# One selection group of four tiles split into two pairs, in a one-core sparse-attention and state-space layer

## The chip, the cores and the metric

The kernel runs on one core of a Trainium2 chip. The time is device microseconds of one execution. The engines are TensorE (PE), VectorE (DVE), ScalarE (ACT), GpSimd (POOL) and SyncE (SP, which here only issues transfers).

## The reference

The layer projects x (4096 rows of 1024) with one matrix. One part of the columns feeds a sparse attention with 8 heads, one a state-space branch; the gated results are projected back, added to x and normalised. What matters here is how the attention picks its keys:

```
idx_logits  = einsum('bthd,bsd->bths', qi, ki)             # 8 index heads of 32
index_score = einsum('bths,bth->bts', relu(idx_logits), wi)
index_score = where(causal, index_score, neg)
_, sel = top_k(index_score, 256)                           # per query
s = where(valid, q_lat . c[sel], neg); p = softmax(s); o = p . c[sel]
```

The kernel doesn't gather. For every query it finds which 256 visible keys have the largest index score, writes a mask of large numbers for all others to DRAM, and the attention adds that mask to dense scores.

## The kernel before

The 4096 queries are 32 tiles of 128. Tile i sees W = 128 (i + 1) keys. The program has four stages: the projections, the selection (which is put in among the projections), the attention with the state-space work beside it, and the output.

**Projections.** x comes in 8 chunks of 512 rows. A sweep multiplies one chunk with the column blocks: first the three blocks that the selection needs, for all chunks, and then, in eight more sweeps, the rest (u, q, two gates). Each of these sweeps ends with "kv", which splits the latent (ch, cl at the tile names qh, ql), makes four k tiles and four v tiles and stores them in eight parts. All these results go through a tile named st with 3 buffers.

**Selection.** `select(group)` (L285 on) takes a group of tiles. It scores each one (`score`: TensorE products of the 8 index heads, L254; ScalarE's relu, L256; VectorE's weighted accumulation into acc, L265), estimates a threshold from mean and spread, and then does 8 rounds (6 for groups of small tiles). In a round every tile of the group is counted once: how many of its scores lie at or above its threshold. A count runs on VectorE (L329, written to a scratch tile mk) or on ScalarE (L325, as a sum of signs, scratch tile junk_a); which engine takes which tile is read from a table of letters, D and A, in `counters`. Then a chain of short VectorE operations on one number a tile (L331 to L367) moves all thresholds of the group together. After the rounds the masks are made, one tile after the other: a sign step on ScalarE (L386), two passes (L390, L391), a maximum (L393) and a match-replace (L401) on VectorE, the mask in pieces of 2048 columns on ScalarE (L405), and its store on SP.

What can overlap is set by buffers: mk and junk_a have one buffer each, acc has four of 4240 columns, into which several tiles of a group are packed, and the small tiles of a group (s_...) have two.

**Order.** The groups run in the order of the list ORDER (L147 to L150). A scheduler that simulates the program fixes the order of the instructions on each engine when the kernel is built; the engines then run them in that order. So a change in a group moves instructions of the sweeps beside it as well. `cm` and `ca` hold, for each tile, the factors that turn a count or a sum of signs into the same quantity; they are filled by the same table.

**After it.** VectorE sums flags that say whether any tile lost a key (L1013 to L1025), TensorE adds them over the lanes (L1027), and all engines read the sum and branch around an exact selection that is only wanted when it isn't zero (L1029, L1030). Attention follows with an order that is written out by hand for PE, DVE and ACT. While the selection ends and once the last sweep has freed its memory, GpSimd prepares the first two batches of the state-space branch (L815 to L863).

Of the kernel before, what the change touches and what calls it, by code (L numbers as in the profile page):

```python
# [71 lines left out]
def tile_hymba(  # L72
# [74 lines left out]
    SMALL = [[2, 3, 4, 5, 6], [7, 8, 9]]  # L147
    MIDDLE = [[i, i + 1, 30 - i, 31 - i] for i in (14, 12)]
    LARGE = [[i, i + 1] for i in range(30, 21, -2)]
    ORDER = SMALL + MIDDLE + LARGE + [[10, 11, 20, 21]]  # L150
    PLACE = {i: k for k, i in enumerate([0, 1] + [i for g in ORDER for i in g])}
    ROOM = P * (NT + 1) + 16
    SB, XB, KB = 2, 5, 8
# [3 lines left out]

    def counters(group, it):
        p = PAT[len(group)]
        return p[it % len(p)]  # L160

    idxs = ctx.enter_context(ExitStack())
    one = idxs.enter_context(tc.tile_pool(name="i_one", bufs=1))
# [28 lines left out]
    DVE.memset(ca, -AIM)  # L192
    for g in ORDER:
        for r in range(2):
            for i, by in zip(g, counters(g, 2 * r)):
                if by == "A":
                    k = slice(PLACE[i], PLACE[i] + 1)
                    POOL.memset(cm[:, r, k], -0.5)
                    POOL.memset(ca[:, r, k], 0.5 * (P * (i + 1)) - AIM)
# [71 lines left out]
    def causal_only(i):  # L271
        W = P * (i + 1)
        m = wk.tile([P, PEN], BF, name="m", bufs=2)
        if W > P:
            DVE.memset(m[:, :W - P], 0.0)
        DVE.tensor_scalar(m[:, W - P:W], capm, 0.0, BIG, op0=OP.is_lt, op1=OP.mult)
        store_mask(i, m, 0, W)
# [13 lines left out]
    def select(group):  # L291
# [29 lines left out]
        for it in range(rounds):  # L321
            for (k, i, v, W), by in zip(tiles, counters(group, it)):
                if by == "A":
                    junk = wk.tile([P, S], mybir.dt.int8, name="junk_a", bufs=1)
                    ACT.activation(junk[:, :W], v[:, :W], AF.Sign, scale=-1.0, bias=th[:, k:k + 1],  # L325
                                   accum_out=ct[:, k:k + 1])
                else:
                    junk = wk.tile([P, PEN], BF, name="mk", bufs=1).bitcast(mybir.dt.uint8)
                    DVE.tensor_scalar(junk[:, :W], v[:, :W], th[:, k:k + 1], None, op0=OP.is_ge, op1=OP.add,  # L329
                                      accum_out=ct[:, k:k + 1])  # L330
# [122 lines left out]
    with ExitStack() as ph:  # L453
# [339 lines left out]
        causal_only(1)  # L793
        for g in ORDER:
            select(g)
# [212 lines left out]
    lost = one.tile([P, NT], FT, name="lost")  # L1008
    NG = len(ORDER)
    lo1 = one.tile([P, NG + 1], FT, name="lo1")  # L1010
# [11 lines left out]
    DVE.tensor_scalar(lost, lost, 0.0625, None, op0=OP.is_gt)  # L1022
    for r, g in enumerate(ORDER):
        DVE.tensor_reduce(lo1[:, r:r + 1], lost[:, PLACE[g[0]]:PLACE[g[0]] + len(g)], axis=AX.X, op=OP.add)
# [5 lines left out]
    with tc.If(n_lost != 0):  # L1030
        for r, g in enumerate(ORDER):
            g_lost = nc.values_load(lo2[:1, r:r + 1], min_val=0, max_val=5 * P)
# [11 lines left out]
    with ExitStack() as ph:  # L1044
# [195 lines left out]
        with tc.manual_schedule(engines={PE_E, DVE_E, ACT_E}):  # L1240
            for n in range(-AHEAD, len(values)):
                if n + AHEAD < len(values):
                    p, b, want = values[n + AHEAD]
# [20 lines left out]
                if n >= 0:  # L1264
                    p, b, _ = values[n]
# [150 lines left out]
```

## Time and profile before

| | us |
|---|---|
| median of 3 runs | 4118.75 (4113.29 to 4124.88) |
| profiled execution | 4111.49 |
| its span | 4109.7 |
| last projection matmul ends | 1667.0 |
| attention's first loads are issued | 1793.4 |

Busy over the span: PE 90%, DVE 80%, ACT 68%, POOL 38%. All times below count from the start of the span. In the page's forty slices, one slice is 102.7 us; the selection and the projections fill the first seventeen and the attention most of the others. A line of the view in order of time gives the start, the duration, the engine, the line of the program, the operation, the tiles it writes and reads, and the shape; in brackets stands how long the engine was idle before and what ended that.

### The profile page before, as it was taken

The numbers are of one execution on the slowest core, as the hardware profiler recorded it, in microseconds if no ns is written. First come the engines' busy times: TensorE is split into PE (matmuls) and PEld (weight loads), VectorE is DVE, ScalarE is ACT, GpSimd is POOL, SyncE is SP. The second block draws the span as 40 slices with busy tenths as digits, with TensorE's granted clock in tenths as the row PEclk, the third lists the DMA queues.
The fourth block names the chain that finished last, engine by engine and source line by source line (L and its number), as shares of the span: only waits on it lengthen the run. The fifth ranks groups of instructions, "written<-read, shape, count | busy, mean of one in ns | idle before, by whom it ended". The sixth has DMA issues, their size and how long they took to land.

```text
span 4109.7 us, 64216 instructions
## 1 busy us (share of the span) xinstructions
PE 3683.6 (90%) x20925; PEld 3111.3 (76%) x20925; DVE 3298.1 (80%) x6879; ACT 2804.1 (68%) x4540; POOL 1545.4 (38%) x3405
## 2 busy tenths in 40 slices
PE   6788988988989989149999999999999999899998
PEld 5566766766757658038888898888898989788887
DVE  5898898888798888778888888888888889565554
ACT  4587878776767776647777777777777778534342
POOL 1110011111111111236665656666656542354543
PEclk9889989989989899569999999999999999999999
DMA  8766967767668677244545444444444444644441
GB/s 226 159 195 177 307 190 213 200 183 221 190 188 230 185 202 203 71 141 117 154 120 149 124 136 137 128 136 127 140 132 135 119 142 121 181 135 134 143 124 72
DMA packets 521898, 656.19 MB, mean 160 GB/s; under 512 B 126800, under 2 KB 367952, under 8 KB 521552
## 3 DMA queue, kind: packets, MB, share of 16 engines
q1 hardware_dynamic: 438800, 448.54, 37.7%
q0 software_dynamic: 82752, 203.45, 18.5%
q8 instruction: 167, 2.74, 0.3%
q14 instruction: 179, 1.47, 0.1%
HBM read 480.61 MB, written 169.13 MB: 158 GB/s over the span
## 4 chain that ended last, share of the span: by engine, by line
PE 45%; ACT 3%; DMA 3%; issue 2%; DVE 2%; POOL 2%; SPq 0%; ACTq 0%; POOLq 0%; DVEq 0%
PE ps_t L1149 10%; PE ps_o L1161 6%; PE ps_o L1162 5%; PE ps_s L1116 5%; PE ps_s L1117 5%; PE ps_y L99 2%; PE ps_y L98 2%; PE ps_y L100 2%; ACT sc L1132 2%; PE ps L959 2%; PE ps_g L99 1%; PE ps_g L100 1%; PE ps_g L98 1%; DMA mb<-mask_d 1%; ACT ph L85 1%
## 5 line engine op out<-in xcount | busy, mean ns | idle before, releaser
L87 DVE TENSOR_TENSOR pl<-ps_t,ph 128x512 fp32r<-128x512 f32 x1088 | 748.5, 689 | 194.2 <-ACT ph L85 181.1
L85 ACT ACTIVATE ph<-ps_t 128x512 fp32r<-128x512 f32 x1088 | 644.2, 596 | 372.6 <-PE ps_t L1149 353.8
L1119 DVE CUSTOM_DVE_ANT_0 sc<-ps_s,mb 128x512 f32<-128x512 f32 (+3 forms) x1152 | 725.6, 638 | 39.2 <-PE ps_s L1117 18.2
L1161 PE MATMUL ps_o<-ph,V 128*128 128x256 f32 x2176 | 659.3, 325 | 29.9 <-ACT ot L1165 27.0
L1149 PE MATMUL ps_t<-ident,sc 128*128 128x128 f32 x4352 | 655.7, 273 | 10.5 <-DVE pl L87 6.0
L256 ACT ACTIVATE relu<-ps_i 128x1024 f32<-128x1024 f32 (+5 forms) x624 | 534.6, 899 | 168.8 <-PE ps_i L254 147.2
L1132 ACT ACTIVATE sc<-sc,mx 128x1024 f32<-128x1024 f32 (+7 forms) x640 | 637.0, 997 | 7.3 <-DVE mx L1119 7.0
L1149 PEld LDWEIGHTS ps_t<-ident,sc 128*128 128x128 f32 x4352 | 537.0, 141 | 122.6 <-DVE pl L87 6.6
L265 DVE SCALAR_TENSOR_TENSOR acc<-relu,wi,acc 128x2048 f32<-128x2048 f32 (+15 forms) x322 | 558.1, 1733 | 77.2 <-ACT relu L256 74.3
L1162 PE MATMUL ps_o<-pl,V 128*128 128x256 f32 x2176 | 565.0, 282 | 2.6 <-DVE pl L87 2.6
L511 POOL DMA_DIRECT2D w<-w_d x294 | 159.0, 541 | 1085.9 <-PE ps_x L100 1005.8
L98 PE MATMUL ps_x<-xk,w 128*128 128x512 f32 x1280 | 517.1, 404 | 6.5 <-DVE st L87 2.0
L100 PE MATMUL ps_x<-xk,w 128*128 128x512 f32 x1280 | 507.3, 396 | 0.0
L99 PE MATMUL ps_x<-xk,w 128*128 128x512 f32 x1280 | 506.5, 396 | 0.0
L254 PE MATMUL ps_i<-kst,qst 128*128 128x512 f32 (+1 forms) x1136 | 394.9, 446 | 117.2 <-ACT relu L256 111.2
L1116 PE MATMUL ps_s<-KT,QH 128*128 128x512 f32 (+2 forms) x1152 | 438.2, 381 | 19.6 <-DMA V<-v_d 15.2
L1161 PEld LDWEIGHTS ps_o<-ph,V 128*128 128x128 f32 x2176 | 413.5, 190 | 47.4 <-ACT ot L1165 39.5
L1117 PE MATMUL ps_s<-KT,QL 128*128 128x512 f32 (+2 forms) x1152 | 436.4, 379 | 0.7 <-DVE QL L87 0.7
L1162 PEld LDWEIGHTS ps_o<-pl,V 128*128 128x128 f32 x2176 | 417.6, 192 | 7.3 <-DVE pl L87 3.3
L254 PEld LDWEIGHTS ps_i<-kst,qst 128*128 128x128 f32 x1136 | 222.1, 213 | 223.9 <-ACT relu L256 185.7
L325 ACT ACTIVATE junk_a<-acc,s_t 128x1920 int8<-128x1920 f32 (+14 forms) x152 | 333.1, 2191 | 53.8 <-DVE s_t L354 24.1
L98 PEld LDWEIGHTS ps_x<-xk,w 128*128 128x128 f32 x1280 | 245.7, 192 | 70.5 <-DMA w<-w_d 6.2
(408 smaller groups left out, 7435.4 us busy)
## 6 DMA issues: line engine op xcount, KB each, us to landing
w<-w_d POOLq DMA_DIRECT2D x294, 512.0 KB, 4.2
mb<-mask_d SPq DMA_DIRECT2D x416, 256.0 KB, 3.1
xs<-in_x_dram SPq DMA_DIRECT2D x120, 256.0 KB, 4.6
w_d<-w SPq DMA_DIRECT2D x42, 512.0 KB, 4.3
qs_d<-st SPq DMA_DIRECT2D x64, 256.0 KB, 3.0
k_d<-st SPq DMA_DIRECT2D x128, 128.0 KB, 2.4
v_d<-st SPq DMA_DIRECT2D x64, 256.0 KB, 3.5
QL<-qT_d SPq DMA_DIRECT2D x64, 256.0 KB, 4.2
```

The costliest lines, as they stand in the source:

```text
L85: ACT.activation(hi, src, AF.Copy, scale=scale)
L87: DVE.tensor_tensor(lo, src, ft(hi), op=OP.subtract)
L98: PE.matmul(ps, lh, rh, start=first, stop=False)
L99: PE.matmul(ps, lh, rl, start=False, stop=False)
L100: PE.matmul(ps, ll, rh, start=False, stop=last)
L1116: PE.matmul(ps[:, :nn], QH[:, qs], kk, start=True, stop=False)
L1117: PE.matmul(ps[:, :nn], QL[:, qs], kk, start=False, stop=True)
L1119: DVE.tensor_tensor_reduce(self.sc[a][-1][:, o], ps[:, :n], self.mb[a][:, o], 1.0, TOP, OP.add, OP.min, mx[:, k:k + 1])
L1132: ACT.activation(v, v, AF.Exp, scale=-1.0, bias=nm, accum_out=self.ds[:, a, r:r + 1])
L1149: PE.transpose(pt[:, e, a, :], self.sc[a][r][:, o:o + P], ident)
L1161: PE.matmul(self.po, v, ph_[:, e, :], start=(b + e == 0), stop=False)
L1162: PE.matmul(self.po, v, pl_[:, e, :], start=False, stop=(b + e == self.nb - 1))
```

## The change

The last group of the selection, of the tiles 10, 11, 20 and 21, becomes two groups, 20 and 21 first and then 10 and 11. `counters` gives both of them the first entry of the table for pairs, "DA", in every round: the first tile of the pair is counted on VectorE, the second on ScalarE. Before, the group of four had "AAAD" in every round: 10, 11 and 20 on ScalarE, 21 on VectorE. Other pairs have "DA", "DA", "AA" in turn.

```
-    ORDER = SMALL + MIDDLE + LARGE + [[10, 11, 20, 21]]
+    ORDER = SMALL + MIDDLE + LARGE + [[20, 21], [10, 11]]
 ...
     def counters(group, it):
         p = PAT[len(group)]
-        return p[it % len(p)]
+        return p[0 if group in ORDER[-2:] else it % len(p)]
```

How this moves instructions is shown at three places. A width of 1408 belongs to tile 10, 1536 to 11, 2688 to 20 and 2816 to 21.

First place, VectorE, the stretch where the last scores of the selection are accumulated. Before, the last accumulation of tile 21 (its last 768 columns) comes ahead of round 0's count:

```order
L265 SCALAR_TENSOR_TENSOR acc<-relu,wi,acc 128x768 x2
L87 TENSOR_TENSOR st<-ps_x,st 128x512
L265 SCALAR_TENSOR_TENSOR acc<-relu,wi,acc 128x768
L87 TENSOR_TENSOR st<-ps_x,st 128x4x64
L266 TENSOR_TENSOR acc<-acc,capm 128x128
L329 TENSOR_SCALAR mk,s_t<-acc,s_t 128x2816
L87 TENSOR_TENSOR st<-ps_x,st 128x4x64
L331 TENSOR_TENSOR s_t<-s_t,cm 128x4
```

Now the last accumulations are tile 11's, and round 1's count of tile 20 stands among them (round 0's is further up, behind the maximum of tile 23):

```order
L354 TENSOR_TENSOR s_t<-s_ab,s_e 128x2
L87 TENSOR_TENSOR st<-ps_x,st 128x4x64
L265 SCALAR_TENSOR_TENSOR acc<-relu,wi,acc 128x1536
L329 TENSOR_SCALAR mk,s_t<-acc,s_t 128x2688
L265 SCALAR_TENSOR_TENSOR acc<-relu,wi,acc 128x1536
L87 TENSOR_TENSOR st<-ps_x,st 128x4x64
L331 TENSOR_TENSOR s_t<-s_t,cm 128x2
L266 TENSOR_TENSOR acc<-acc,capm 128x128
L304 BN_STATS s_st<-acc 128x6
L332 TENSOR_TENSOR s_t<-s_t,ca 128x2
L87 TENSOR_TENSOR st<-ps_x,st 128x4x64 x2
```

The splits of the v parts (L87, 128x4x64) stand between the short operations of a round in both orders, round 0's before and round 1's now.

Second place, VectorE, from the masks of tiles 20 and 21 into the rounds of 10 and 11, in the changed kernel. Before, no count stands behind a mask pass here:

```order
L401 MATCH_REPLACE acc<-s_top,acc 128x2696
L391 TENSOR_TENSOR acc<-acc,mk 128x768
L393 MAX s_top<-acc 128x8
L329 TENSOR_SCALAR mk,s_t<-acc,s_t 128x1408
L397 TENSOR_TENSOR eq_114<-s_top 128x7
L331 TENSOR_TENSOR s_t<-s_t,cm 128x2
L398 SCALAR_TENSOR_TENSOR s_eqj,tf<-slot_111,s_e,eq_114 128x8
L400 COPY_PREDICATED s_top<-s_tm,spare 128x8
L332 TENSOR_TENSOR s_t<-s_t,ca 128x2
L401 MATCH_REPLACE acc<-s_top,acc 128x2824
```

Round 0 of the small pair begins inside the masks of the large one; its other rounds follow behind them.

Third place, ScalarE, the end of the selection. Before, the last round and the masks of four tiles:

```order
L325 ACTIVATE junk_a,s_t<-acc,s_t 128x1408
L325 ACTIVATE junk_a,s_t<-acc,s_t 128x1536
L325 ACTIVATE junk_a,s_t<-acc,s_t 128x2688
L386 ACTIVATE acc<-acc,s_sg 128x1408
L386 ACTIVATE acc<-acc,s_sg 128x1536
L386 ACTIVATE acc<-acc,s_sg 128x2688
L386 ACTIVATE acc<-acc,s_sg 128x2816
L405 ACTIVATE m,fl<-acc,s_bi,s_sc 128x1408
L405 ACTIVATE m,fl<-acc,s_bi,s_sc 128x1536
```

Now:

```order
L325 ACTIVATE junk_a,s_t<-acc,s_t 128x2816 x6
L325 ACTIVATE junk_a,s_t<-acc,s_t 128x1536
L386 ACTIVATE acc<-acc,s_sg 128x2688
L386 ACTIVATE acc<-acc,s_sg 128x2816
L405 ACTIVATE m,fl<-acc,s_bi,s_sc 128x2048
L405 ACTIVATE m,fl<-acc,s_bi,s_sc 128x640
L405 ACTIVATE m,fl<-acc,s_bi,s_sc 128x2048
L405 ACTIVATE m,fl<-acc,s_bi,s_sc 128x768
L325 ACTIVATE junk_a,s_t<-acc,s_t 128x1536 x7
L386 ACTIVATE acc<-acc,s_sg 128x1408
L386 ACTIVATE acc<-acc,s_sg 128x1536
```

Seven of tile 11's eight counts stand behind the four mask pieces of tiles 20 and 21. Behind the branch the order on PE and ACT is the same in both.

## Rows read from the trace of the kernel before

**Rows 1.** The page: its head, TensorE's share, and TensorE in forty slices.
```profile
span 4109.7 us, 64216 instructions
PE 3683.6 (90%) x20925; PEld 3111.3 (76%) x20925; DVE 3298.1 (80%) x6879; ACT 2804.1 (68%) x4540; POOL 1545.4 (38%) x3405
PE   6788988988989989149999999999999999899998
```

**Rows 2.** TensorE in order of time, from the last projection to the flags.
```profile
1666.37 0.63 PE L100 MATMUL ps_x<-w,ql 128*128 128x512 f32 x1
1787.18 0.20 PE L1027 MATMUL ps_i<-lo,ones 128*1 128x11 f32 x2 [120.18 <-DVE lo L1025]
```

**Rows 3.** VectorE in order of time: counts of rounds 0 to 3, one later round.
```profile
1667.48 3.15 DVE L329 TENSOR_SCALAR_CACHE_REDUCE mk<-acc,s_t 128x2816 uint8<-128x2816 f32 x1
...
1684.42 3.13 DVE L329 TENSOR_SCALAR_CACHE_REDUCE mk<-acc,s_t 128x2816 uint8<-128x2816 f32 x1
...
1694.22 3.15 DVE L329 TENSOR_SCALAR_CACHE_REDUCE mk<-acc,s_t 128x2816 uint8<-128x2816 f32 x1
...
1703.00 3.15 DVE L329 TENSOR_SCALAR_CACHE_REDUCE mk<-acc,s_t 128x2816 uint8<-128x2816 f32 x1
...
1719.20 3.15 DVE L329 TENSOR_SCALAR_CACHE_REDUCE mk<-acc,s_t 128x2816 uint8<-128x2816 f32 x1
...
1725.21 0.16 DVE L331 TENSOR_TENSOR s_t<-s_t,cm 128x4 f32<-128x4 f32 x1 [2.86 <-ACT junk_a L325]
...
1727.30 3.15 DVE L329 TENSOR_SCALAR_CACHE_REDUCE mk<-acc,s_t 128x2816 uint8<-128x2816 f32 x1
```

**Rows 4.** ScalarE in the same later round: tiles 11 and 20, last reading.
```profile
1720.85 1.57 ACT L325 ACTIVATE junk_a<-acc,s_t 128x1536 int8<-128x1536 f32 x1
1722.33 0.19 ACT L325 ACTIVATION_READ_ACCUMULATOR junk_a<-acc,s_t 128x1 f32 x1
1722.55 2.54 ACT L325 ACTIVATE junk_a<-acc,s_t 128x2688 int8<-128x2688 f32 x1
1724.99 0.19 ACT L325 ACTIVATION_READ_ACCUMULATOR junk_a<-acc,s_t 128x1 f32 x1
```

**Rows 5.** VectorE: the last round's count, first mask steps, last match-replace.
```profile
1735.39 3.15 DVE L329 TENSOR_SCALAR_CACHE_REDUCE mk<-acc,s_t 128x2816 uint8<-128x2816 f32 x1
...
1742.29 0.17 DVE L372 TENSOR_SCALAR s_m<-s_ab 128x4 f32<-128x4 f32 x1
...
1744.33 0.95 DVE L390 TENSOR_SCALAR mk<-acc,s_t 128x1408 bf16<-128x1408 f32 x1 [0.38 <-ACT acc L386]
...
1776.66 3.08 DVE L401 MATCH_REPLACE8 acc<-s_top,acc 128x2824 f32<-128x2824 f32 x1
```

**Rows 6.** ScalarE: the four sign steps, the end of the last mask.
```profile
1742.83 7.89 ACT L386 ACTIVATE acc<-acc,s_sg 128x1408 f32<-128x1408 f32 x4 [1.46 <-DVE s_sg L379]
...
1782.83 0.19 ACT L405 ACTIVATION_READ_ACCUMULATOR m<-acc,s_bi,s_sc 128x1 f32 x1
```

**Rows 7.** VectorE by line and shape up to 1790 us: busy us, mean ns.
```profile
L329 DVE TENSOR_SCALAR_CACHE_REDUCE mk<-acc,s_t 128x2560 uint8<-128x2560 f32 x8 | 23.0, 2878 | 0.2
...
L265 DVE SCALAR_TENSOR_TENSOR acc<-relu,wi,acc 128x640 f32<-128x640 f32 x14 | 12.3, 880 | 7.0 <-ACT relu L256 6.9
...
L329 DVE TENSOR_SCALAR_CACHE_REDUCE mk<-acc,s_t 128x1152 uint8<-128x1152 f32 x6 | 8.4, 1406 | 0.1
```

**Rows 8.** Last sweep: ScalarE's split of the latent, VectorE's last v split.
```profile
1647.39 0.63 ACT L85 ACTIVATE qh<-st 128x512 fp32r<-128x512 f32 x1 [2.18 <-DMA st<-c_d]
...
1690.43 0.42 DVE L87 TENSOR_TENSOR st<-ps_x,st 128x256 fp32r<-128x256 f32 x1
```

**Rows 9.** GpSimd and VectorE beside each other; busy us from 1675 to 1700.
```profile
1674.68 2.34 POOL L817 TENSOR_TENSOR U<-U,Uh 128x1024 fp32r<-128x1024 f32 x1
1674.71 2.40 DVE L344 SCALAR_TENSOR_TENSOR s_ab<-s_t,s_e 128x4 f32<-128x4 f32 x2
...
1675.00:1700.00 25.00, 0.00 (x0) 0.00 (x0) 19.37 (x39) 12.54 (x15) 14.02 (x16) 0.50 0.18 52
```

**Rows 10.** The same view: PE, PEld, DVE, ACT, POOL, clock, DMA share, GB/s.
```profile
1500.00:1600.00 100.00, 86.87 (x340) 66.03 (x341) 78.09 (x145) 70.30 (x83) 12.94 (x23) 0.91 0.68 183
```

## The prediction

> **What bounds the kernel now.** I read the page first. Its span is 4109.7 us, TensorE is busy for 90% of it, and its forty slices stand at 6 to 9 tenths except for one, the seventeenth, with 1 [rows 1]. That hole is the place of this change: the last projection matmul runs at 1666.37, and the next thing TensorE does is the small sum over the loss flags at 1787.18, after 120 us of waiting for VectorE [rows 2]. Attention can't begin before a branch that reads those flags, so every microsecond of the selection's end is on the path. What fills the hole is read on VectorE and ScalarE in order of time. The last group of four tiles counts eight rounds: counts on VectorE begin at 1667.48, 1684.42, 1694.22, 1703.00 and then every 8.10 us [rows 3]. In each round ScalarE is the longer side (tiles 10, 11 and 20 one after the other; VectorE's count of tile 21 is over sooner), and then a chain of short VectorE operations, 2.09 us from 1725.21 to 1727.30, moves the thresholds [rows 3, 4]. After round 7 the masks are made: 1742.29 to 1783.02, mostly VectorE with one tile after the other [rows 5, 6].
>
> **The change part by part.** The rounds get shorter, but there are twice as many, and the order on VectorE and ScalarE says that the two pairs don't overlap: all of pair 20/21's rounds come first, then its masks, and the first count of tile 10 stands behind tile 20's match-replace and tile 21's maximum; ScalarE has seven of its eight counts of tile 11 behind the four mask pieces of 20 and 21. Each count on VectorE writes a scratch tile of one buffer (mk) that the masks use too, and each count on ScalarE another of one buffer, so the next group can't count while this one does. I therefore add the pairs up in sequence.
>
> Count times: VectorE takes 1.406 us for 1152 columns and 2.878 for 2560, so 1.045 ns a column: 1.67 for tile 10 (1408) and 3.01 for tile 20 (2688) [rows 7]. ScalarE takes 1.70 for tile 11 from start to start, and 2.63 for 2688 columns with the reading of the sum [rows 4]; tile 21's 2816 are 2.74.
> - A round of 20/21: VectorE is longer, 3.01 and 0.1 to its reading, then the chain 2.09: 5.2 us.
> - A round of 10/11: both sides about 1.78, chain 2.09: 3.87 us.
> - Round 2 has 0.7 us more of short operations (8.78 against 8.10), round 1 about 0.9 (an estimate: the same five operations in one chain), and after round 7 the way to the masks is 1.2 shorter (6.90 from 1735.39 to 1742.29) [rows 3, 5].
>
> From the start of round 2's count of the last large tiles, before: 48.1 us to the masks, and 40.7 for them, 88.8 in all [rows 3, 5, 6]. After, on the same path:
> - rounds 2 to 7 of 20/21: 6 x 5.2 + 0.7 - 1.2 = 30.7;
> - masks: the VectorE work from the first is-ge to the end of the last match-replace is the same 35.4 (1744.33 to 1779.74), now in two pieces, each with a start that waits for ScalarE's sign step. For tile 10 that is 2.0, as before; for tile 20 it is 3.1, since its 2688 columns are 2.5 of the 7.9 us of the four [rows 5, 6];
> - round 0 of 10/11 inside the masks of tile 21: the count 1.7 and 0.3 of short operations. Then ScalarE must write tile 21's mask, 3.4 us (the 3.3 from the end of the match-replace to the end of the last piece, and a gap), before it can count tile 11 again [rows 5, 6]; the 17 short operations of round 0, 2.7 us at 0.16 each, lie beside that [rows 3];
> - rounds 1 to 7 of 10/11: 7 x 3.87 + 0.9 + 0.7 - 1.2 = 27.5;
> - the last mask, of tile 11, one piece of 1536 columns that I take at its count's 1.70 and a gap: 1.8, where tile 21's two pieces took 3.3 [rows 4].
> Sum: 30.7 + 3.1 + 35.4 + 2.0 + 2.0 + 3.4 + 27.5 + 1.8 = 105.9. That is 17.1 us more than before, if round 2 of the large pair starts when it did.
>
> It starts somewhat earlier, which is where the change gains. Rounds 0 and 1 of 20/21 are now counted while tiles 10 and 11 are still being scored: the new order has round 0 right behind the masks of 22/23, and round 1 seven eighths through tile 11's accumulations. Before, rounds 0 and 1 took 26.7 us in the open (1667.48 to 1694.22) [rows 3]. But they are not free. Round 1's chain stands on VectorE behind the splits of the last sweep's v tiles; the last of them began 43.0 us after that sweep's latent was split (1647.39 to 1690.43) [rows 8], since each waits for a store to free one of three buffers. And the accumulations now stand later: where the masks of 22/23 begin, the old order has already scored 1408 + 1536 + 2688 + 512 columns a head and the new one 2688 + 2816, so 640 columns times eight heads, 8 x 0.88 = 7.0 us of VectorE, are still to do at that point [rows 7]. Going down the new order from there by the durations of the old run, I get the last v split at 1685 to 1691 and round 2 some 2.5 us behind it, by its twelve or so short operations. I take 1691 for round 2, 3 us earlier than before, so the net is 17.1 - 3 = **14 us slower**. The bounds of this term: the old chain of round 0 held up the last v splits by at most the 8.8 us that it was longer than a later round (16.9 against 8.1) [rows 3]. Without that they end at 1682, round 2 starts at 1684, and 5 us sooner if the 7.0 us above were not needed in the open: 1679, or +2. The other end is 1701, +24, from GpSimd:
>
> When the sweep frees its memory, GpSimd prepares the first state-space batches; it was busy for 14.0 of the 25 us from 1675. Short VectorE operations beside it stretch: two at L344, four numbers a lane, took 2.40 together while a GpSimd subtraction took 2.34 [rows 9]. A count, with one tensor input, took 3.13 beside GpSimd at 1684.42, no longer than at 1719.20 without it [rows 3]. In the new order the GpSimd operations meet accumulations of tile 11 (L265, two tensor inputs) and round 1's chain instead of round 0's. In the 1691 I have counted 4 us of their 14 as exposed, the rest beside VectorE's wait for the v splits; all 14 exposed is 1701. The Trainium skill (GPSIMD Engine Reference, 1. Specifications) says that GpSimd's SBUF interfaces are shared with VectorE and contend with its instructions that have two SBUF inputs. The rows of L344 agree; by that rule the long accumulations are hit too, which is the upper end just given.
>
> The skill (VectorE: DVE Perf Modes, Mode 2×_2P) also has a rule that speaks against my round: an operation on one fp32 tensor with a scalar may read through both ports, two results a cycle. The is-ge at L390 does (0.95 us for 1408 columns), the count at L329 does not (1.12 ns a column) [rows 3, 5]. If the count of 2688 columns were halved, ScalarE would set the round, 4.9 instead of 5.2, and the sum fall by 2 us; the row decides.
>
> Behind the branch PE and ScalarE have the same order as before, so I cost the rest at nothing. One more group in the flags is one more short reduce. GpSimd's spread for 10/11 (L307) now stands among its state-space operations, but its result is wanted only after the masks of 20 have begun, and SP's mask stores are in the order of the masks: nothing for either. Everything ahead of the masks of 22/23 is reordered too, since the scheduler reacts to each shift; the trace can't price that. In the 100 us from 1500, TensorE was busy 86.9 and VectorE 78.1 us [rows 10], so there is slack that a new order can gain or lose; I allow 8 us either way.
>
> **Its own time.** The profiled execution took 4111.49 us, 1.8 more than its span and 7.3 below the median of the runs, 4118.75. On its terms the forecast is 4125.5; against the median, with the same 14 us, 4132.
>
> **Rivals.**
> 1. *The large pair is hidden altogether.* Round 2 starts by 1683: the v splits go faster without the old chain in front of them. For it: the old stall of 8 us in that chain. Against: 43 us for the sweep's end, which is no VectorE matter alone. Price: +2 to +6, 4121 to 4125 against the median.
> 2. *Faster, because scoring ends sooner.* With 20 and 21 scored first, the remaining scores are short tiles whose work fits between the sweep's matmuls; the stretch to 1667 shrinks. Break-even is round 2 at 1677, a gain past 0.3% needs it before 1665. For it: the idle tenths of TensorE in the first sixteen slices [rows 1]. Against: the sweep's matmuls are unchanged and all 22/23 work stands in front as before. Price: about -15, 4104.
> 3. *GpSimd and the accumulations in turn.* All 14 us of GpSimd work fall between VectorE operations: round 2 at 1701, +24, 4143. For it: VectorE has no pause in that part of the new order. Against: its waits for the v splits, 16.9 us of stretch and wait together before [rows 3].
> 4. *The pairs overlap after all*, so that one's chain lies beside the other's count. A double round would be about 3.1 + 1.8 + 2.1 = 7 us, six of them 42 instead of 48, masks 2 longer, the start 3 earlier: -7, 4112. The written order speaks against it on both engines.
>
> **How the numbers follow.** Forecast 0.60 (its own range +6 to +22), rival 1 0.17, rival 2 0.08, rival 3 0.12, rival 4 0.03. A difference below 0.3%, 12.4 us, can't be told from none. Slower by more: the part of the forecast above 12.4 us, six tenths of it, 0.36, and rival 3, so 0.48. Within: 0.24 + 0.17 + 0.03 = 0.44. Faster: 0.08. The range reaches from -6 to +28 around the median, 4113 to 4147: it leaves out rival 2 and the far end of rival 3.
>
> **What would show it.** In the profile after: VectorE counts of 2688 columns 5.2 us apart and then, some 31 us after the last of them began, counts of 1408 columns 3.9 us apart; two separate stretches of match-replace; TensorE idle from its last projection for 130 to 140 us instead of 120; round 2 of the large pair near 1691. I am wrong if counts of the two pairs alternate, if that round starts before 1680, or if the last projection matmul moves by more than 10 us from 1666.

## The result and the profile after

The changed kernel takes 4141.9 us (median of six runs, 4131.91 to 4149.21), the kernel before 4116.1 beside it: ratio 1.0061, interval 1.0044 to 1.0079. A second set of six, run for e13 below, gives 1.0077 (1.0061 to 1.0092). The forecast, 14 us slower, has the right sign and is too small: 26 to 33 us are lost. The range, -6 to +28 us, holds the first set and not the second (+33). The runs of one kernel spread over up to 25 us (before: 4105.85 to 4131.15 in 35 runs), so a single trace is read here for its durations and distances, and the size of an effect is taken from the ratios.

The page of the changed kernel: its span, TensorE's busy time, its forty slices and the granted clock, which answer to [rows 1].

```profile
span 4139.2 us, 64329 instructions
PE 3682.5 (89%) x20925; PEld 3109.1 (75%) x20925; DVE 3325.0 (80%) x7009; ACT 2792.6 (67%) x4524; POOL 1554.1 (38%) x3403
...
PE   6788988988989889129999999999999999799998
...
PEclk9898998998989889559999999999999999899999
```

The hole is now in two slices, the seventeenth and the eighteenth, 1 and 2 tenths, and the granted clock stands at 5 tenths of full speed (1.2 GHz) in both. TensorE's rows on both sides of it, in order of time (start, duration, engine, line, operation, tiles, shape; in brackets the idle time before and what ended it):

```profile
1677.21 0.98 PE L254 MATMUL ps_i<-kst,qst 128*128 128x512 f32 x3 [0.91 <-ACT relu L256]
...
1811.14 0.20 PE L1027 MATMUL ps_i<-lo,ones 128*1 128x12 f32 x2 [132.94 <-DVE lo L1025]
```

The small sum over the flags comes 24.0 us later than in [rows 2], and the last score matmul ahead of the hole ends 11 us behind the old last projection. VectorE's counts and the first step of the flags, the answer to [rows 3] and the end of [rows 5]:

```profile
1699.30 3.01 DVE L329 TENSOR_SCALAR_CACHE_REDUCE mk<-acc,s_t 128x2688 uint8<-128x2688 f32 x1
...
1707.23 3.01 DVE L329 TENSOR_SCALAR_CACHE_REDUCE mk<-acc,s_t 128x2688 uint8<-128x2688 f32 x1
...
1712.41 3.01 DVE L329 TENSOR_SCALAR_CACHE_REDUCE mk<-acc,s_t 128x2688 uint8<-128x2688 f32 x1
...
1767.65 1.68 DVE L329 TENSOR_SCALAR_CACHE_REDUCE mk<-acc,s_t 128x1408 uint8<-128x1408 f32 x1
...
1772.16 1.68 DVE L329 TENSOR_SCALAR_CACHE_REDUCE mk<-acc,s_t 128x1408 uint8<-128x1408 f32 x1
...
1787.56 1.68 DVE L329 TENSOR_SCALAR_CACHE_REDUCE mk<-acc,s_t 128x1408 uint8<-128x1408 f32 x1
...
1806.95 0.19 DVE L1013 TENSOR_TENSOR fl<-fl 128x32 f32<-128x32 f32 x1 [1.83 <-ACT m L405]
```

Counts of 2688 columns stand 5.19 us apart from round 3 on (once 5.55), and behind all of them come those of 1408 columns, 3.85 apart from their round 3 on: two pairs in sequence, as forecast. From round 2 (1699.30) to the flags (1806.95) it is 107.65 us; the forecast's sum was 105.9, before it was 88.8. What went wrong lies ahead of round 2: it starts 5.1 us later than before and not 3 earlier. The second trace of the changed kernel (e13 below; the order of every engine is the same) says how far a position can be trusted. From round 2 to the flags it has 107.61 us, but the last sweep's latent is split 7.3 us later in it (1659.97 against 1652.67), round 2 starts at 1707.78, and the last projection matmul is at 1679.21, 12.8 us behind [rows 2] where the first trace has 6.3 (1672.64). The second is beyond the 10 us that the prediction named as a sign of being wrong.

So two questions are open. Is the sequence itself the loss, and what makes it one (e1, e2, e4, e11, e12)? And why is everything ahead of it late (e5, e6, e7, e10)? The first theory was: one scratch buffer puts the pairs in sequence, +18; a reorder of the scheduler's adds some 5; GpSimd beside VectorE the rest.

### The profile page after: what moved, and what is told of

It is laid out like the page before. It is cut to its first block, busy times and chain, and to the rows that moved or that the text cites. A ratio compares the mean times of both kernels' runs of the same rounds, so it can differ in the third digit from the quotient of the medians.

```text
span 4139.2 us, 64329 instructions
## 1 busy us (share of the span) xinstructions
PE 3682.5 (89%) x20925; PEld 3109.1 (75%) x20925; DVE 3325.0 (80%) x7009; ACT 2792.6 (67%) x4524; POOL 1554.1 (38%) x3403
## 3 DMA queue, kind: packets, MB, share of 16 engines
q1 hardware_dynamic: 438800, 448.54, 37.4%
## 4 chain that ended last, share of the span: by engine, by line
PE 46%; ACT 3%; DMA 2%; DVE 2%; issue 2%; POOL 1%; SPq 0%; ACTq 0%; POOLq 0%; DVEq 0%
PE ps_t L1149 10%; PE ps_o L1161 6%; PE ps_o L1162 5%; PE ps_s L1116 5%; PE ps_s L1117 5%; PE ps_y L99 2%; PE ps_y L100 2%; PE ps_y L98 2%; ACT sc L1132 2%; PE ps L959 2%; PE ps_g L98 1%; PE ps_g L99 1%; PE ps_g L100 1%; ACT ph L85 1%; DMA mb<-mask_d 1%
## 5 line engine op out<-in xcount | busy, mean ns | idle before, releaser
L87 DVE TENSOR_TENSOR pl<-ps_t,ph 128x512 fp32r<-128x512 f32 x1088 | 749.1, 689 | 196.1 <-ACT ph L85 182.7
L85 ACT ACTIVATE ph<-ps_t 128x512 fp32r<-128x512 f32 x1088 | 643.5, 596 | 374.2 <-PE ps_t L1149 356.3
L325 ACT ACTIVATE junk_a<-acc,s_t 128x1920 int8<-128x1920 f32 (+15 forms) x144 | 322.5, 2240 | 75.7 <-DVE s_t L354 33.8
```

Source lines behind the costliest of these rows:

```text
L85: ACT.activation(hi, src, AF.Copy, scale=scale)
L87: DVE.tensor_tensor(lo, src, ft(hi), op=OP.subtract)
```

## The experiments

All ratios are to the kernel before, run on the same chip beside each.

### The letters: e1 and e2

e1 is the changed kernel with the letters of the other pairs:

```
-        return p[0 if group in ORDER[-2:] else it % len(p)]
+        return p[it % len(p)]
```

> The changed kernel with one part undone: the two pairs stay, but they take the letters of the other pairs, DA, DA, AA in turn, so that in rounds 2 and 5 both tiles of a pair are counted on ScalarE. Theory (the loss is the second pair's own rounds in sequence; the letters DA help): an AA round of 20/21 is 2.63 + 2.74 of counting and 2.1 of chain, 7.5 us against the 5.19 measured, of 10/11 1.6 + 1.7 and 2.1, 5.5 against 3.85, so two of each make it (2.3 + 1.6) x 2 = 8 us longer than the changed kernel, about 33 us above before (ratio near 1.008). Rival (the letters are what costs, because VectorE is loaded with counts that ScalarE had): faster than the changed kernel by up to that much, near 1.004. Look at the distance between the counts of rounds 2 and 5.

Measured: 1.0038 (1.0023 to 1.0053), faster than the changed kernel. Yet the rounds are as the theory has them: large counts of rounds 4 and 6 begin at 1702.52 and 1715.25, so the AA round between took 7.5 us, and the small pair's took 5.4. It lost 8 us there and gained more ahead of it: the last sweep's latent is split at 1641.00 against 1652.67. What the letters have to do with that was unknown at this point; e7 answers it.

e2 leaves one group of four and evens out its letters:

```
-        return p[it % len(p)]
+        return "DADA" if group == ORDER[-1] else p[it % len(p)]
```

> The kernel before with one group of four, and only the letters evened out, DADA: 10 and 20 on VectorE, 11 and 21 on ScalarE. Theory (the pairs cost, the even letters help): a round is 1.67 + 3.01 + 0.1 of counts on VectorE, with ScalarE's 1.70 + 2.74 beside them, and a chain of 2.1: 6.9 us against 8.1, so six rounds give 7 us back; round 0 and 1 stand where they stood, and the time is 7 to 8 us below before, ratio 0.998. Rival (the letters make VectorE, which also does the splits, later): rounds 0 and 1 move back by the two more counts, 4.7 us each, and eat the gain: ratio 1.000 to 1.001.

Measured: 1.0000 (0.9990 to 1.0009). VectorE's first counts of two rounds:

```profile
1721.77 1.68 DVE L329 TENSOR_SCALAR_CACHE_REDUCE mk<-acc,s_t 128x1408 uint8<-128x1408 f32 x1
...
1728.71 1.68 DVE L329 TENSOR_SCALAR_CACHE_REDUCE mk<-acc,s_t 128x1408 uint8<-128x1408 f32 x1
```

The round is 6.94 us, as expected, against 8.10 in [rows 3]. But the last latent split is at 1660.02, 12.6 us behind [rows 8], which is more than six such rounds give. So here, too, something far ahead of the rounds moved.

### The scratch: e4

The counts of 10/11 write to the free end of that pair's own acc tile.

```
+        own.clear()
+        if group == ORDER[-1]:
+            own.extend(rooms[0][0][:, k:k + 400].bitcast(t) for k, t in ((2976, mybir.dt.int8), (3376, mybir.dt.uint8)))
 ...
-                    junk = wk.tile([P, S], mybir.dt.int8, name="junk_a", bufs=1)
+                    junk = own[0] if own else wk.tile([P, S], mybir.dt.int8, name="junk_a", bufs=1)
```

(and own[1] in the place of mk for VectorE's count)

> The changed kernel, but the counts of the pair 10/11 write to scratch of their own (1600 bytes a lane each for VectorE and ScalarE, in the free end of that pair's acc room), so that the two pairs need not wait for each other's scratch. The written order now has counts of 2688 and 1408 columns in turn on VectorE, and both chains beside each other from round 4 on. Theory (one scratch buffer puts the pairs in sequence, but VectorE is the longer side in both, so a double round is still 3.0 + 1.67 + two chains of 2.1 = 8.9 us against 5.19 + 3.85 = 9.0): the rounds gain next to nothing, only the wait of round 0 of 10/11 for the masks of 20/21 goes (about 5 us), so 5 to 8 us below the changed kernel, ratio near 1.0045 to before. Rival (what the scratch serializes is worth the whole loss: a double round of 7 us, as rival 4 of the prediction had it): six double rounds 42 instead of 58, and the wait gone too, about 20 us below the changed kernel, ratio near 1.001. Rival two: two chains beside each other cost hardly more than one, since each short operation waits for the one before it; then a double round is 6.8 and the result is the same as the first rival's.

Measured: 1.0010 (1.0000 to 1.0021), 20 us below the changed kernel. Here are VectorE's rows of one double round; lines have moved by five (L334 is the count, L336 to L359 the chain):

```profile
1733.39 3.01 DVE L334 TENSOR_SCALAR_CACHE_REDUCE mk<-acc,s_t 128x2688 uint8<-128x2688 f32 x1
...
1736.59 1.67 DVE L334 TENSOR_SCALAR_CACHE_REDUCE acc<-acc,s_t 128x1408 uint8<-128x1408 f32 x1
...
1738.72 0.17 DVE L351 COPY_PREDICATED s_ab<-s_b,s_t 128x8 f32<-128x8 int32 x1
1738.81 0.16 DVE L338 TENSOR_SCALAR s_b<-s_t 128x2 int32<-128x2 f32 x1
1738.88 0.16 DVE L339 TENSOR_SCALAR s_b<-s_t 128x2 int32<-128x2 f32 x1
1738.94 0.16 DVE L354 TENSOR_TENSOR s_d<-s_ab 128x4 f32<-128x4 f32 x1
1739.07 0.17 DVE L351 COPY_PREDICATED s_ab<-s_b,s_t 128x8 f32<-128x8 int32 x1
1739.16 0.16 DVE L355 RECIPROCAL s_e<-s_d 128x2 f32<-128x2 f32 x1
...
1740.15 3.01 DVE L334 TENSOR_SCALAR_CACHE_REDUCE mk<-acc,s_t 128x2688 uint8<-128x2688 f32 x1
```

Counts of both pairs alternate, 6.76 us from one of 2688 columns to the next. The theory's 8.9 is wrong and rival two right: the two chains, 22 short operations, take 6.76 - 3.01 - 1.67 - 0.16 = 1.9 us together, less than the 2.1 of a single chain of 11 in [rows 3]. The rows show how: the operations of one chain stand between those of the other and start 0.06 to 0.13 apart. So the sequence was the scratch buffer's doing. In this trace the way from round 2 to the flags is 1791.96 - 1707.03 = 84.9 us, 22.7 less than in the changed kernel.

### What a reorder is worth: e6, e10 and e7

e6 is the kernel before with `[11, 10, 20, 21]` for `[10, 11, 20, 21]`.

> The kernel before with the last group written [11, 10, 20, 21]: the same work on the same engines, but the scheduler writes another order from the point where these tiles are scored. It sizes what a reorder by itself does. Theory (the last sweeps come 5 us later in the changed kernel because of the order alone, which falls either way): between -5 and +5 us, ratio 0.999 to 1.001, with the last projection matmul up to 6 us away from 1666.4. Rival (a reorder is worth nothing, and those 5 us belong to the earlier scoring of 20 and 21): ratio 1.000 within 0.0005 and the last projection matmul within 1 us.

Measured: 0.9991 (0.9982 to 1.0001). The last projection matmul is 5.9 us later than in [rows 2] (1672.23), and the sum over the flags 0.8 (1787.99): a shift of this size ahead of the hole need not reach its end, and the time does not show it. The matmul lies outside the rival's 1 us, but two traces of one order differ by more (1672.64 and 1679.21 above), so one trace does not decide between the two. What the interval shows is that a reorder this late is worth less than 0.2%.

The traces of after, e2 and e4 differ from those of before, e1 and e6 much earlier. ScalarE's first split of a latent (L85, qh) in the kernel before and in the changed one, with the last one of the latter:

```profile
504.91 0.67 ACT L85 ACTIVATE qh<-st 128x512 fp32r<-128x512 f32 x1
```

```profile
509.96 0.69 ACT L85 ACTIVATE qh<-st 128x512 fp32r<-128x512 f32 x1
...
1652.67 0.64 ACT L85 ACTIVATE qh<-st 128x512 fp32r<-128x512 f32 x1
```

(e2: 513.65, e4: 514.96; e1: 503.53, e6: 503.32.) The two sets have another trait in common. In the setup every tile that ScalarE counts in rounds 0 or 2 gets two columns set by GpSimd, at L198 and L199. The letters DA in both pairs, and DADA, need four of these memsets fewer; AAAD, and the letters in turn, need twelve. GpSimd's written order there, before (-) and in the changed kernel (+):

```
 L215 IOTA z 128x1 x7
-L198 MEMSET cm 128x1
-L199 MEMSET ca 128x1
-L198 MEMSET cm 128x1
-L199 MEMSET ca 128x1
 L215 IOTA z 128x1 x23
 ...
-L511 DMA w<-w_d 128x1024 x2
-L244 DMA qst<-qs_d 128x8x128
-L511 DMA w<-w_d 128x1024
+L511 DMA w<-w_d 128x1024 x3
```

From there the scheduler's order differs on all engines (TensorE from its 314th matmul on, 109 us into the span, where score matmuls move). All fourteen traces sort by the number of these memsets. The first split is at 502.8 to 507.4 in the eight with twelve and at 510.0 to 515.0 in the six with eight. The last one is at 1639.4 to 1643.6 against 1652.7 to 1660.0 in the kernels with two pairs, and at 1646.7 to 1652.3 against 1655.1 to 1660.0 in those with a group of four. e10 takes the four away from the kernel before, by setting neighbouring columns at once; its projections then have the changed kernel's order.

```
-                    POOL.memset(cm[:, r, k], -0.5)
+                    if i not in (10, 11):
+                        POOL.memset(cm[:, r, k.start - 2 * (i == 20):k.stop], -0.5)
```

> The kernel before, with the same values written to its factor tables by four memsets fewer (three neighbouring columns at once instead of one by one). Nothing else is changed; the written order of the projections becomes that of the changed kernel. Theory (the order that follows from four fewer memsets costs by itself): 5 to 10 us slower than before, ratio 1.0012 to 1.0025, the first latent split 5 to 10 us after 504.9 and the last one 5 to 12 after 1647.4. Rival (single runs differ by that much and the order is worth nothing): ratio 1.000 within 0.001.

Measured: 1.0014 (1.0002 to 1.0025), with the splits

```profile
511.46 0.68 ACT L85 ACTIVATE qh<-st 128x512 fp32r<-128x512 f32 x1
...
1655.12 0.62 ACT L85 ACTIVATE qh<-st 128x512 fp32r<-128x512 f32 x1
```

6.6 and 7.7 us late, and the flags' sum at 1795.26, 8.1 late. The theory holds. e7 is the other direction: the changed kernel with the four memsets repeated, so that its projections have the old order.

```
+                    if i in (11, 21):
+                        POOL.memset(cm[:, r, k], -0.5)
```

> The changed kernel with four GpSimd memsets repeated in the setup, so that there are as many as before (the letters DA need four fewer than AAAD, since only tiles counted on ScalarE get one). With that the written order of all engines is the old one again up to where tiles 20 and 21 are scored; in the changed kernel it differs from the first projection blocks on. Theory (the changed kernel's sweeps are 5 to 12 us late because four memsets in the setup gave the scheduler another order, as in the runs e2 and e4, whose first latent splits come 9 and 10 us after before's, while e1, with the old number of memsets, is 1.4 us ahead): the first split within 2 us of 504.9, the whole about 10 to 15 us below the changed kernel, ratio 1.002 to 1.004. Rival (e1 was faster than the changed kernel because of its letters, not of its setup): no change against the changed kernel, ratio 1.006.

Measured: 1.0018 (1.0007 to 1.0030), 4125.85 us, just below the theory's 1.002. The first split is at 507.43, 2.5 us from before's and not within 2, though the order on TensorE, VectorE and ScalarE is the same up to there. e13 repeats the changed kernel to hold against it.

> The changed kernel itself once more, on the same chip as the others of this set, since its first six runs leave an interval of 1.0044 to 1.0079 and the price of the setup is its distance to e7 (1.0018). Theory (order of the setup 6 to 18 us, pairs 7): ratio 1.004 to 1.006. Rival (the first runs were high by chance, the setup costs nothing in this kernel): 1.002 to 1.003.

Measured: 1.0077 (1.0061 to 1.0092). It is above both ranges, so nothing was high by chance in the first six. The setup's order costs the changed kernel 0.4 to 0.6%, some 17 to 24 us, more than the kernel before (e10, 6). Why this order is the worse one, and why it costs the pairs more, no run shows. ScalarE, VectorE and TensorE in e7 (two lines of code more ahead of L300, so L331 is the count):

```profile
1642.07 0.64 ACT L85 ACTIVATE qh<-st 128x512 fp32r<-128x512 f32 x1
```

```profile
1690.00 3.01 DVE L331 TENSOR_SCALAR_CACHE_REDUCE mk<-acc,s_t 128x2688 uint8<-128x2688 f32 x1
...
1695.84 3.01 DVE L331 TENSOR_SCALAR_CACHE_REDUCE mk<-acc,s_t 128x2688 uint8<-128x2688 f32 x1
```

```profile
1799.52 0.21 PE L1029 MATMUL ps_i<-lo,ones 128*1 128x12 f32 x2 [130.41 <-DVE lo L1027]
```

Round 2 of the large pair starts at 1690.00 (forecast: 1691), and the flags come 12.3 us later than before (forecast: 14). So what I priced is the kernel with the old setup. Its time is closer to before than the forecast, though: 1.0018 is 7 us (3 to 12), and the traced run was 4 us above the median of its set.

### GpSimd beside VectorE: e5

The preparation of the state-space batches reads a zero that VectorE writes only behind the flags (the first line below follows L1025, and L815 adds the same zero); the order on the other engines stays that of the changed kernel.

```
+    DVE.tensor_scalar(zeros2, lo1[:, NG:], 0.0, None, op0=OP.mult)
 ...
+            POOL.tensor_tensor(self.pk, self.pk, zeros2[:, :, None].to_broadcast([P, GH, NPK]), op=OP.add)
```

> The changed kernel, with its own setup, but GpSimd's preparation of the state-space batches waits for the flags (its operands pass through a zero that is written behind L1025). The order on TensorE, VectorE and ScalarE stays that of the changed kernel. Theory (GpSimd beside the last accumulations and the chain of round 1 costs 7 to 9 us): accumulations of 1.81 us throughout, round 2 of the large pair at 1690 to 1692 instead of 1699.3 if the last latent split is where it was, 38 us behind it instead of 46.6; L1027 as much sooner; after the branch GpSimd's 28 us stand ahead of the attention's first loads, so the whole is no faster. Rival (the wait for the v stores sets that stretch and GpSimd only fills it): round 2 stays 45 to 47 us behind the last latent split.

The same stretch on VectorE in the changed kernel, with GpSimd beside it:

```profile
1679.89 3.27 DVE L265 SCALAR_TENSOR_TENSOR acc<-relu,wi,acc 128x1536 f32<-128x1536 f32 x1
1683.08 3.00 DVE L329 TENSOR_SCALAR_CACHE_REDUCE mk<-acc,s_t 128x2688 uint8<-128x2688 f32 x1
...
1686.01 2.24 DVE L265 SCALAR_TENSOR_TENSOR acc<-relu,wi,acc 128x1536 f32<-128x1536 f32 x1
...
1688.51 1.51 DVE L331 TENSOR_TENSOR s_t<-s_t,cm 128x2 f32<-128x2 f32 x1
...
1690.75 1.69 DVE L332 TENSOR_TENSOR s_t<-s_t,ca 128x2 f32<-128x2 f32 x1
...
1695.26 0.65 DVE L352 TENSOR_SCALAR s_e<-s_e 128x2 f32<-128x2 f32 x1
```

and in e5 without:

```profile
1683.24 1.81 DVE L265 SCALAR_TENSOR_TENSOR acc<-relu,wi,acc 128x1536 f32<-128x1536 f32 x1
1684.97 3.00 DVE L329 TENSOR_SCALAR_CACHE_REDUCE mk<-acc,s_t 128x2688 uint8<-128x2688 f32 x1
...
1687.90 1.81 DVE L265 SCALAR_TENSOR_TENSOR acc<-relu,wi,acc 128x1536 f32<-128x1536 f32 x1
...
1689.97 0.15 DVE L331 TENSOR_TENSOR s_t<-s_t,cm 128x2 f32<-128x2 f32 x1
...
1690.84 0.14 DVE L332 TENSOR_TENSOR s_t<-s_t,ca 128x2 f32<-128x2 f32 x1
...
1693.58 0.17 DVE L352 TENSOR_SCALAR s_e<-s_e 128x2 f32<-128x2 f32 x1
...
1695.55 3.01 DVE L329 TENSOR_SCALAR_CACHE_REDUCE mk<-acc,s_t 128x2688 uint8<-128x2688 f32 x1
...
1701.39 3.01 DVE L329 TENSOR_SCALAR_CACHE_REDUCE mk<-acc,s_t 128x2688 uint8<-128x2688 f32 x1
```

The accumulation is 1.81 us instead of 3.27 and 2.24, the two operations on two numbers 0.15 and 0.14 instead of 1.51 and 1.69, and L352, which has one tensor input, 0.17 instead of 0.65. The count ahead took 3.00 both times. Round 2 starts 40.3 us behind the split of the last latent (1655.22) instead of 46.6 (47.8 in the second trace), and takes 5.84 instead of 7.93: 8.4 us in all, within the theory's 7 to 9, though the distance alone had been put at 38. The theory's last point did not come, since nothing was given back: attention's first matmul follows the flags' sum by 17.11 us (16.84 in the changed kernel), although GpSimd did four of the delayed operations ahead of attention's loads and the others among them. The one run took 4131.4 us, below every run of the changed kernel (lowest 4131.91; median 4147.18 on the same chip, e13), with before at 4113.95 beside it; a single run is no interval.

### Which pair first, and the best version: e11, e8, e9, e12

e11 is e7 with `[[10, 11], [20, 21]]`.

> The two pairs in the other order, 10/11 first, letters DA, with the four memsets repeated (the order of the projections is that of before). Compare with e7. Theory (pairs in sequence, whichever comes first): the sum has 5 or 6 rounds of 3.85 and 7 of 5.19 in the open instead of 6 of 5.19 and 7 of 3.85, about 1 us less to 1 us more, and the last mask is two pieces, +1.6; ratio 1.001 to 1.003. Rival (the small pair's rounds vanish under the scoring of 20/21 and the splits, since their counts are short): six rounds of 3.85 hidden more, 15 us below e7, ratio 0.998.

Measured: 1.0048 (1.0031 to 1.0064). The rival, which said faster, is out; but the theory's range is missed as well, and the interval lies above e7's (1.0007 to 1.0030), by 0.3% or some 12 us. The trace doesn't show where they go: its flags begin at 1794.44, in e7 at 1795.33, but the profiled run was the fastest of its six, 9 us below their median. So whether it matters which pair comes first stays open. One thing the trace does show, the last latent split:

```profile
1640.47 0.64 ACT L85 ACTIVATE qh<-st 128x512 fp32r<-128x512 f32 x1
```

It is as early as in e7 (1642.07), although tiles 20 and 21 are scored last here.

e8 is e2 with the memsets repeated as in e7.

> One group of four with the letters DADA, and the four memsets repeated, so that the order of the projections is that of before. Theory (the letters give 6 to 7 us in the rounds, measured 6.94 apart in e2 against 8.10, and e2 lost them to the order that fewer memsets gave): 6 to 8 us below before, ratio 0.998 to 0.9985. Rival (VectorE's longer share of the first two rounds beside the splits eats the gain, and the setup is worth nothing): ratio 1.000 as e2.

Measured: 0.9991 (0.9978 to 1.0004). The rounds are 6.93 us, and round 2 starts at 1696.62, 2.4 later than in [rows 3], since VectorE's two counts stand in rounds 0 and 1 as well: both the theory and its rival are in it, and a gain is not shown.

e9 is e4 with the memsets repeated.

> The changed kernel with scratch of its own for the counts of 10/11 (as e4) and the four memsets repeated. Theory (scratch and setup are two separate costs that add): 8 to 15 us below e4's 4121.7, so 4107 to 4114, ratio 0.9975 to 0.9995. Rival (the setup's order is worth nothing, or what it gives is taken by a wait for GpSimd or the last v stores): ratio 1.001 as e4.

Measured: 0.9982 (0.9970 to 0.9995), 4108.51 us, inside the theory's range. The scratch gives 0.36% here (against e7) and 0.51% with the changed kernel's setup (e4 against its first set), so the two costs add in the main. This kernel is faster than the one before, by 0.05 to 0.3%. Its flags' sum:

```profile
1783.65 0.20 PE L1034 MATMUL ps_i<-lo,ones 128*1 128x12 f32 x2 [113.59 <-DVE lo L1032]
```

e12 is e4 with AA for 10/11; its projections have the old order without any repeat.

```
-        return p[0 if group in ORDER[-2:] else it % len(p)]
+        return "AA" if group == ORDER[-1] else p[0 if group == ORDER[-2] else it % len(p)]
```

> As e4 and e9 (scratch of its own for the counts of 10/11), but both tiles of 10/11 are counted on ScalarE, AA, and 20/21 stay DA. The number of memsets is then that of before without repeating any, and so is the order of the projections. Theory (with the pairs side by side VectorE is the longer side: 3.0 + 1.67 + 0.2 of counts and 1.85 of the two chains, 6.75 measured; without the 1408 columns it is 5.0, and ScalarE with 2.76 + 1.60 + 1.70 becomes the longer one, 6.1): six double rounds of 6.1, 4 us below e9's 4108.5, ratio 0.9965 to 0.9985. Rival (the chain of 10/11 then stands alone behind ScalarE's counts, 3.3 + 2.1 after 2.76): double rounds of 7.5 to 8, 5 us above e9, ratio 0.9995.

Measured: 1.0004 (0.9992 to 1.0016). The theory's range is missed; the ratio is 0.2% above e9's, with intervals that just meet. ScalarE's counts of tile 10 late in the selection (L330 here):

```profile
1750.43 1.45 ACT L330 ACTIVATE acc<-acc,s_t 128x1408 int8<-128x1408 f32 x1
...
1755.82 1.47 ACT L330 ACTIVATE acc<-acc,s_t 128x1408 int8<-128x1408 f32 x1 [2.15 <-DVE s_t L359]
...
1761.23 1.47 ACT L330 ACTIVATE acc<-acc,s_t 128x1408 int8<-128x1408 f32 x1 [2.15 <-DVE s_t L359]
```

The large pair's rounds are 5.2 and 6.5 us in turn, so it ran ahead, and three rounds of the small pair stand alone behind its masks, 5.4 us each: the rival's price (3.3 and 2.1), in another place than it said.

## Why the prediction was right in sign and short in size

- **Two pairs in sequence, +17: right.** 107.65 us from round 2 to the flags against 105.9 forecast; e7 has 105.33. The 2 us more are GpSimd in round 2 (7.93 against 5.84 in e5). In e7 the terms are right one by one: rounds of the large pair 30.8 (forecast 30.7), starts of the masks 3.1 and 2.0 (the same), VectorE's mask work with round 0 of the small pair in it 37.3 (37.4), the wait for tile 21's mask 3.2 (3.4), the other rounds of the small pair 27.1 (27.5), the last mask 1.8 (1.8). The round of the large pair is 5.19 (forecast 5.2), of the small 3.85 (3.87). The cause given, the scratch of one buffer, is shown by e4: without it the sequence goes, and 20 us with it.
- **Round 2 starts at 1691, 3 us earlier: wrong for this kernel, by 8 us (17 in its second trace).** The term that failed is the one that I set to nothing with 8 us either way, what the scheduler does to everything ahead. It is 6 us with the old last group (e10) and 17 to 24 with the pairs (e7 against both sets of the changed kernel). With the old setup round 2 does start at 1690.00. The diff removes four memsets in the setup by way of the letters, and I followed the letters only to the rounds.
- **GpSimd, 4 of its 14 us exposed: too small.** e5 gives 8.4. The end of 1691 came out in e7 all the same, because there the last latent is split 5.3 us earlier than before (1642.07 against 1647.39). The prediction had no term for this gain. It comes with the two pairs (1639.4 to 1643.6 in all five traces with the old setup, 1646.7 to 1652.3 in the three of a group of four), and not with scoring 20 and 21 first, since e11 has it too. It is about what GpSimd took beyond the 4 us, so the two errors cancel, and the hit on 1691 is luck.
- **GpSimd's ports.** The accumulation with two tensor inputs was stretched from 1.81 to 3.27 us, and the count with one kept its 3.00 in both traces. The Trainium skill (GPSIMD Engine Reference, 1. Specifications) names VectorE instructions with two SBUF inputs as ones that contend with GpSimd, and so far the trace agrees. The same row also names instructions in a two-port mode, which the prediction left out. A short operation with one tensor input, L352, was stretched too (0.65 us instead of 0.17); whether it ran in such a mode no run here shows.
- **The double rate for a count: out, as the row said.** The count of 2688 columns takes 3.00 us, 1.12 ns a column; the rule of the Trainium skill (VectorE: DVE Perf Modes, Mode 2×_2P) is not seen on it.
- **Nothing behind the branch: nearly.** Attention's first matmul follows the flags' sum by 16.84 us instead of 15.37; over all traces it is 16.3 to 17.8 with two pairs and 13.8 to 15.8 with a group of four. From the start of the flags to the end of the span the changed kernel took 5.6 us longer than before (7.0 in its second trace) and e7 6.1 longer. But e4, with two pairs, took no longer than before, and e6, with a group of four, 4.4 longer, so what isn't the 1.5 us is not shown to come from the change.
- **The range.** That the first set's 4141.9 lies inside it is partly luck. Its upper end, +28 us, lies 4 above the dearest case that was priced (+24, all of GpSimd's work exposed). Most of the loss came from a reorder of 17 to 24 us, for which 8 had been allowed; without it the kernel loses 7 (3 to 12), not 14.
- **Rivals.** The overlap of rival 4 was priced well (7 us a double round, 6.76 measured) but needs the second scratch. Rival 3 had the time of the result, 4143, for another reason: GpSimd's whole share is 8.4 us, not 14.

## What to carry to other kernels

When a table is changed that a scheduler reads, look for every place that loops over the table, the setup too: a few tiny operations fewer there can give all later stages another order, and that order can cost more than the edit itself. To price an edit apart from such a reorder, pad the setup until the old order comes back, and time that. And before work is cut into groups that should overlap, count the buffers of their scratch: one buffer is a sequence, whatever the engines could do.

## What the runs showed of the hardware

- Short VectorE operations start further apart when each needs the result of the one before: 11 in one chain take 2.09 us, 0.19 each [rows 3], while 22 of two chains in turn take 1.9 us, 0.09 each (e4).
- VectorE and GpSimd hold each other up both ways. L331 on two numbers took 1.51 us instead of 0.15. Two of GpSimd's operations were hit as well (rows of the changed kernel, with one of VectorE's accumulations ahead):

```profile
1675.83 1.81 DVE L265 SCALAR_TENSOR_TENSOR acc<-relu,wi,acc 128x1536 f32<-128x1536 f32 x1
...
1675.91 1.86 POOL L863 TENSOR_SCALAR co<-pk 128x14 f32<-128x14 f32 x1
...
1683.74 0.25 POOL L863 TENSOR_SCALAR co<-pk 128x14 f32<-128x14 f32 x1
...
1679.64 1.90 POOL L815 TENSOR_TENSOR Uh<-U,zeros 128x1024 fp32r<-128x1024 f32 x1
...
1686.59 3.41 POOL L815 TENSOR_TENSOR Uh<-U,zeros 128x1024 fp32r<-128x1024 f32 x1
```

The same L863 takes 1.86 and 0.25 us, the same L815 1.90 and 3.41. The slow L863 lies beside an accumulation (1675.83 to 1677.64) and ends just behind it; the quick one lies beside the count (1683.08 to 1686.08). The slow L815 lies beside the accumulation of 2.24 us at 1686.01.
